# Windowed attention by 32 queries of four heads, with ACT, DVE and POOL in written order: one change to a fused trunk kernel on Trainium2

## The chip, the core and the metric

The kernel runs on one core of a Trainium2 chip as one launch. The core has a matrix engine (PE), a vector engine (DVE), a scalar engine (ACT), GpSimd (POOL) and SyncE (SP, here a queue that issues DMAs). The metric is the device time of an execution in microseconds, the median of several. A profile shows one execution; its span runs from the first to the last instruction, and a time "at 88.31" is counted from the start of the span.

## What is computed

One layer of a model with 512 positions and width 2048: a root-mean-square norm, attention in a window of 128 keys with 32 query heads of width 64 on 4 key and value heads, a bias by distance, one "sink" logit per head, a gate, an output projection, and then a gated embedding and a last norm.

```python
q, k, v, gate = jnp.split(h @ w_in, [2048, 2304, 2560], axis=-1)
...
scores = jnp.einsum('bnqhgd,bnjhd->bnhgqj', q, kb) * (64 ** -0.5) + bias
scores = jnp.where(mask, scores, jnp.finfo(jnp.float32).min)
m = jnp.maximum(scores.max(axis=-1, keepdims=True), sink)
e = jnp.exp(scores - m)
probs = e / (e.sum(axis=-1, keepdims=True) + jnp.exp(sink - m))
out = jnp.einsum('bnhgqj,bnjhd->bqhd', probs, vb)
...
x = x + (out * silu(gate)) @ w_out
x = x + (p @ ple_proj) * sigmoid(rmsnorm(x, ple_norm) @ ple_gate)
return rmsnorm(x, final_g)
```

## The kernel before

Matrices are multiplied in float32 split into a high part (rounded to the matrix engine's 4-byte format by a copy on ACT) and a low part (the rest, by a subtraction on DVE). `mm3` then issues three matmuls: high by high, high by low, low by high.

The stages follow each other on PE. First comes a loop of 16 steps over the width, which makes the first two query tiles, the keys and the values. Then 30 projections follow: 14 query tiles (two heads each) and 16 gate tiles, 16 steps of three matmuls each. Their weights come in 60 halves of 8 steps (half 0 to half 59; `wraw` is a half as loaded, `whi` and `wlo` its parts). `Weights.get(i)` makes the halves up to i + 2 as soon as half i is used, and `_make` loads a half by a DMA on SP's queue and splits it. Three buffers of each kind exist. The third stage, the output projection and the gate of the embedding by a scheme of seven products (`unit`), and the end are touched by one line only (`early`, which says after which step of `unit` a half of the last weights is split by `split_last`).

Attention is spread over the projections. The first projection stands ahead of it; then there are 64 blocks, 8 (`g`) for each of 8 groups of four heads (`d`). Turn i of the loop issues on PE the transposes of block i - 2 (`turn`), the weighing of the values of block i - 3 (`weigh`), the scores of block i (`scores`), and then about seven steps of the projections. A block before is 64 queries of two heads on the 128 partitions, twice (for the two pairs of heads), against 192 keys, or 128 in the first two blocks of a group. The keys lie as a high and a low half side by side, so a score matmul has 2 x 192 columns. `add` scales the product and adds the bias; of 192 keys a query sees 128, and since the two outer thirds exclude each other (the bias masks one), a maximum folds them together. Then come the maximum, the exponential with its sum, the reciprocal and the product with it.

Because keys of two blocks are folded, `weigh` needs beside the values V a second product: the masked weights (`own`) by differences of neighbouring value tiles (DV). `make_diff(n)` forms difference n on POOL and splits it by `split`; `spread_diff(n)` copies it into DV by four DMAs on SP's queue. `first_chores` does all three `make_diff` in turn 0, and in turns 1 to 3 the split of V[i] and `spread_diff(i)`. `own` is masked on POOL from the transposed weights `r`, and half of it is copied by ACT (the last line of `turn`). `weigh` ends every second block with two copies on ACT (`tmp`), each followed by an add on DVE.

Who sets the order: PE, SP and (in the attention) POOL run in the order in which the code is written. ACT and DVE have their instructions ordered by a scheduler before the kernel runs, apart from the stretch called `seam` and the end. On the chip each engine then runs its list in order. DMAs on SP's queue are issued in list order; one whose source isn't ready holds up all behind it. In that queue stand, at the start of attention: the bias of group 0, halves 3 and 4, a copy for `sum_weights`, spread 1, half 5, spread 2, half 6, and so on.

Of the kernel before, what the change touches and what calls it, by code (L numbers as in the profile page):

```python
# [19 lines left out]
S = 512  # L20
P = 128
# [9 lines left out]
UNITS = S // HB  # L31
BUCKETS = 32
# [7 lines left out]
PAD = 32  # L40
# [13 lines left out]
def trunk_kernel(ctx: ExitStack, tc: tile.TileContext, a: dict):  # L54
# [32 lines left out]
    class Weights:  # L87
# [4 lines left out]

        def add(self, src):
            self.srcs.append(src)
# [30 lines left out]
    sinkb = const.tile([P, PAIRS], F32, name="sinkb")  # L125
# [17 lines left out]
    sclq = const.tile([P, UNITS], F32, name="sclq")  # L143
# [24 lines left out]
    q_at = {int(0.5 + 3.516 * (c // 2)) - 2 + c % 2: c for c in range(2, PAIRS)}  # L168
# [15 lines left out]

    for k in range(KC):
        both = start_pool.tile([P, 2, 768], F32R, tag="w0s", name=f"w0s{k}")
# [50 lines left out]
        if k == 9:  # L237
            run(rsqrt_mean(rstd1, ssq1, D, "r1"))
            for e in range(2):
                for b in range(2):  # L240
                    nc.vector.tensor_scalar_mul(
                        sclq[HB * e : HB * e + HB].rearrange("p (n b) -> p n b", b=2)[:, :, b],
                        rstd1[HB * b : HB * b + HB], HD ** -0.5,
                    )

            rdram = tc.dram_tile([NB, P], F32, name="rdram")
            nc.gpsimd.dma_start(rdram.rearrange("t p -> p t"), rstd1)
            nc.gpsimd.dma_start(rb, rdram.rearrange("t p -> (t p)").partition_broadcast(P))
        if k == 10:
            for e in range(2):  # L250
                nc.sync.dma_start(sinkb[HB * e : HB * e + HB], a["sinks"][e].partition_broadcast(HB))
            nc.sync.dma_start(pn, a["ple_norm"])
# [5 lines left out]
    def evac_q(c, ps):  # L258

        q = Q[c] = kvq.tile([P, UNITS, 2, HB], F32R, tag="q", name=f"q{c}", bufs=4)  # L260
        halves = slice(0, 64), slice(64, 128)
        for e in range(2):
            src = ps[halves[e]].rearrange("p (g q) -> p g q", q=HB)
            hi, lo = q[halves[e], :, e], q[halves[1 - e], :, e]
            nc.scalar.copy(hi, src)
            nc.vector.tensor_sub(lo, src, hi.bitcast(F32))


    seam = ExitStack()
    seam.enter_context(  # L270
        tc.manual_schedule(engines={getattr(mybir.EngineType, v) for v in ("PE", "SP", "DVE", "Activation")})
    )
    for c in range(2):
        evac_q(c, q_ps[c])
# [4 lines left out]
    def make_key(h):  # L279

        t, e = divmod(h, 2)
        k = K[h] = kvq.tile([P, 2, S], F32R, tag="k", name=f"k{h}", bufs=2)
        same = slice(64 * e, 64 * e + 64)
        for o in (slice(0, 64), slice(64, 128)):
            nc.scalar.copy(k[o, 0], kt[t][same])
        for o in (slice(0, 64), slice(64, 128)):
            nc.vector.tensor_sub(k[o, 1], kt[t][same], k[same, 0].bitcast(F32))
# [4 lines left out]
    def split(dst, v):  # L292
        nc.scalar.copy(dst[:, :, 0, :], heads(v))
        nc.vector.tensor_sub(dst[:, :, 1, :], heads(v), dst[:, :, 0, :].bitcast(F32))

    nc.vector.tensor_mul(kt[0], kt_ps[0], rb)
    make_key(0)
# [8 lines left out]
    split(V[0], values[0])  # L306
    seam.close()
# [29 lines left out]
    DV = apool.tile([P, NB - 1, 2, KVH * 2 * HD], F32R, name="DV")  # L337
    diffs = {}

    def make_diff(n):  # L340
# [8 lines left out]
        split(dst.rearrange("p (h l d) -> p h l d", h=KVH, l=2), v)  # L349
# [7 lines left out]
    def first_chores(i):  # L357
        if i == 0:
            for n in range(1, NB):
                make_diff(n)  # L360
        if 1 <= i < NB:
            split(V[i], values[i])
            spread_diff(i)

    def load_bias(d):
        biases[d] = apool.tile([P, 2, P + HB], F32, tag="bias", name=f"bias{d}", bufs=2)
        for e in range(2):
            src = bass.AP(
                tensor=tdram.tensor, offset=tdram.offset + (4 * d + e) * TOEP + HB,
                ap=[[1, HB], [2 * TOEP, 2], [1, P + HB]],  # L370
            )
            nc.sync.dma_start(biases[d][HB * e : HB * e + HB], src)

    def scores(i):

        d, g = divmod(i, UNITS)
        odd = g % 2
# [4 lines left out]
        first = max(g - 2, 0) * HB  # L384
        n = P if g < 2 else P + HB
        s_ps = spsum.tile([P, 2, S], F32, tag="w", name=f"s{i}")
        for u in range(2):
            st = Q[2 * d + u][:, g].rearrange("p e q -> p (e q)")
            nc.tensor.matmul(s_ps[:, u, : 2 * n], st, key[:, :, first : first + n], start=True, stop=True)
        t = apool.tile([P, 2, 4 + P + HB], F32, tag="t", name=f"t{i}", bufs=4)  # L390
        seen = t[:, :, 65:194] if odd else t[:, :, 0:129]
        pr = t[:, :, 65:193] if odd else t[:, :, 1:129]
        sink = 193 if odd else 0
        nc.gpsimd.tensor_copy(t[:, :, sink], sinkb[:, 2 * d : 2 * d + 2])
        bias = biases[d][:, :, ::-1]

        def add(out, in0, in1):
            nc.vector.scalar_tensor_tensor(
                out=out, in0=in0, scalar=sclq[:, g : g + 1], in1=in1, op0=ALU.mult, op1=ALU.add
            )  # L400

        if g < 2:
            if g == 0:
                nc.gpsimd.memset(t[:, :, 65:129], MASKED)
            n = HB * (g + 1)
            out = pr[:, :, :n]
            add(out, s_ps[:, :, :n], bias[:, :, 192 - n :])
            add(out, s_ps[:, :, P : P + n], out)
        else:
            add(t[:, :, 1:193], s_ps[:, :, :n], bias)  # L410
            add(t[:, :, 1:193], s_ps[:, :, n : 2 * n], t[:, :, 1:193])
            ends = t[:, :, 1:65], t[:, :, 129:193]
            nc.vector.tensor_max(ends[odd], ends[0], ends[1])
        sm = apool.tile([P, 24], F32, tag="sm", name=f"sm{i}", bufs=4)
        nc.vector.tensor_reduce(sm[:, 0:2], seen, axis=AX.X, op=ALU.max, negate=True)  # L415
        for u in range(2):
            su = seen[:, u, :]
            nc.scalar.activation(su, su, AF.Exp, bias=sm[:, u : u + 1], accum_out=sm[:, 2 + u : 3 + u])  # L418
        nc.vector.reciprocal(sm[:, 4:6], sm[:, 2:4])
        for u in range(2):  # L420
            nc.scalar.mul(pr[:, u], pr[:, u], sm[:, 4 + u : 5 + u])
        T[i] = pr

    def turn(i):
# [5 lines left out]
        for u in range(2):  # L430
            nc.tensor.transpose(pt[:, u * P : (u + 1) * P], pr[:, u, :], ident)
        r = apool.tile([P, 2, 256], F32R, tag="r", name=f"r{i}", bufs=2)
        nc.scalar.copy(r[:, 0], pt)
        nc.vector.tensor_sub(r[:, 1], pt, r[:, 0].bitcast(F32))  # L434
        own = None
        if g >= 2:
# [9 lines left out]
            )  # L446
            here, there = slice(HB, P), slice(0, HB)
# [3 lines left out]
        PT[i] = (r, own)  # L451

    def weigh(i):
# [14 lines left out]
        if own is not None:  # L468
            nc.tensor.matmul(
                out, DV[:, n - 1, b, kv * 2 * HD : (kv + 1) * 2 * HD], own[:, 0], start=False, stop=True  # L470
            )
        if b:
# [5 lines left out]
        if g == UNITS - 1:  # L478
            for c in (2 * d, 2 * d + 1):
                weighed.add(c)  # L480
                if c in open_gates:
                    due.append(c)

    weighed, open_gates, due = set(), set(), []
    ah, al = {}, {}

    def gate_value():

        c = due.pop(0)
# [5 lines left out]
    def open_gate(c, ps):  # L495
# [3 lines left out]
        nc.vector.tensor_mul(x, ps, rb)  # L499
        nc.scalar.activation(ps, x, AF.Tanh, scale=0.5)  # L500
        nc.vector.scalar_tensor_tensor(out=x, in0=ps, scalar=1.0, in1=x, op0=ALU.add, op1=ALU.mult)
        open_gates.add(c)
        if c in weighed:
            due.append(c)
# [183 lines left out]
    def projections():  # L688
        for m, (kind, c) in enumerate(kinds):
            ps = bank(f"{kind}ps{c}", "p")  # L690
            for k in range(KC):
# [6 lines left out]
                if k == KC - 1:  # L698
                    if kind == "q":
                        evac_q(c, ps)  # L700
                    else:
                        g = c // 4
                        if c % 4 == 0:
                            gates[g] = quarter(f"gate{g}")
                        open_gate(c, ps)
# [3 lines left out]

    during = ExitStack()  # L710
    during.enter_context(
        tc.manual_schedule(engines={getattr(mybir.EngineType, v) for v in ("PE", "SP", "Pool")})
    )
    load_bias(0)
    for _ in range(KC):
        next(proj)
    blocks = TWOS * UNITS
    left = KC * (len(kinds) - 1)

    for i in range(blocks + 3):  # L720

        if 2 <= i < blocks + 2:
            turn(i - 2)
        if 3 <= i:
            weigh(i - 3)
        if i < blocks:
            scores(i)
            first_chores(i)
            if i in (6, 20, 36):
                make_key(1 + i // 16)  # L730
# [11 lines left out]
    while due:  # L742
        gate_value()
# [210 lines left out]
    early = {(5, 0, 3): 0, (5, 1, 2): 1, (5, 1, 3): 2, (3, 0, 1): 3, (3, 0, 3): 4, (3, 1, 0): 5, (3, 1, 2): 6}  # L954
# [161 lines left out]
def laid_out(i):  # L1116
# [24 lines left out]
        "sinks": f(np.asarray(i["swa_sinks"])[0].reshape(PAIRS, 2).T),  # L1141
# [19 lines left out]
```

## Time and profile before

| | |
|---|---|
| Median of 3 executions | 803.88 us (803.66 to 804.14) |
| The profiled execution: its own time | 804.26 us |
| Its span | 802.4 us |
| Mean granted clock of the matrix engine | 0.996 |
| First step loop, about | 4.7 to 72.4 us |
| Attention and projections, about | 72.4 to 449 us |
| DVE and ACT busy from 100 to 440 us | 261 and 226 of 340 us |

On the timeline a row gives the start, the duration, the engine, the line, the operation, output <- input, the shape and how many instructions are merged (x2); brackets show the idle time ahead and what ended it. Matmuls overlap, so their cost is the distance of their starts. A row of a group gives line, engine, operation, tiles, shape, count, then the busy time in us and the mean of one in ns, then the engine's idle time just before and what ended it. A row of DMA issues gives count, size of one and the median of us from issue to landing.

### The profile page before, as it was taken

Reading aid. Unit: us, or ns where it says so; the run is one execution under the profiler, and the core shown is the slowest. Engines: PE = TensorE matmul, PEld = TensorE weight load, DVE = VectorE, ACT = ScalarE, POOL = GpSimd, SP = SyncE. Lnnn points to the kernel's source line nnn. Section 1 sums busy time; section 2 is a strip of 40 time slices with the busy share of each in tenths; the row PEclk is TensorE's granted clock in tenths of the full one; section 3 lists DMA queues with packets and bytes.
Section 4 is the critical chain, followed back from the end, with each engine's and each line's share of the span. In section 5 each row is a group of like instructions: output and inputs, shape, how many; then the busy total and the mean of one; then the engine's idle time right before and its main releaser. Section 6 shows DMA issues by size and latency. Waiting matters only on the chain. (4 is left out here: it accounts for less than half of the span.)

```text
span 802.4 us, 10946 instructions
## 1 busy us (share of the span) xinstructions
PE 791.1 (99%) x3763; PEld 660.0 (82%) x3763; DVE 592.1 (74%) x970; ACT 500.5 (62%) x1041; POOL 110.1 (14%) x218
## 2 busy tenths in 40 slices
PE   9999999999999999999999999999999999999995
PEld 7888888888888888888888888888888888888785
DVE  4536886887777776777778897766646756989896
ACT  5624667676667666676666654655668656656855
POOL 0002213122122212112122200030000020200000
PEclk9999999999999999999999999999999999999998
DMA  8863678778687977868685369898513996785532
GB/s 318 327 172 101 183 241 215 228 202 233 172 220 215 218 215 199 221 177 246 159 219 132 105 233 348 333 275 248 195 46 92 372 216 197 156 229 182 182 107 105
DMA packets 45239, 165.15 MB, mean 206 GB/s; under 512 B 5936, under 2 KB 8112, under 8 KB 41344
## 3 DMA queue, kind: packets, MB, share of 16 engines
q1 hardware_dynamic: 38352, 130.59, 47.9%
q0 software_dynamic: 6832, 33.88, 22.4%
q8 instruction: 29, 0.48, 0.2%
q14 instruction: 26, 0.21, 0.1%
HBM read 158.63 MB, written 46.19 MB: 255 GB/s over the span
## 5 line engine op out<-in xcount | busy, mean ns | idle before, releaser
L576 DVE TENSOR_TENSOR blo<-braw,bhi 128x1024 fp32r<-128x1024 f32 x80 | 97.5, 1222 | 39.7 <-ACT bhi L575 39.4
L575 ACT CAST bhi<-braw 128x1024 fp32r<-128x1024 f32 x80 | 84.0, 1051 | 65.8 <-PE g L122 18.9
L122 PE MATMUL gps<-xh,wlo 128*128 128x512 f32 x256 | 100.1, 391 | 0.0
L121 PE MATMUL gps<-xl,whi 128*128 128x512 f32 x256 | 100.1, 391 | 0.0
L120 PE MATMUL gps<-xh,whi 128*128 128x512 f32 x256 | 99.8, 390 | 0.0
L107 DVE TENSOR_TENSOR wlo<-wraw,whi 128x1024 fp32r<-128x1024 f32 x60 | 73.3, 1221 | 20.8 <-ACT whi L106 19.7
L122 PE MATMUL qps<-xh,wlo 128*128 128x512 f32 x224 | 87.8, 392 | 0.0
L120 PE MATMUL o<-bhi,fho 128*128 128x512 f32 x224 | 87.7, 391 | 0.0
L121 PE MATMUL qps<-xl,whi 128*128 128x512 f32 x224 | 87.7, 391 | 0.0
L121 PE MATMUL o<-blo,fho 128*128 128x512 f32 x224 | 87.3, 390 | 0.0
L122 PE MATMUL o<-bhi,flo 128*128 128x512 f32 x224 | 87.2, 389 | 0.0
L120 PE MATMUL qps<-xh,whi 128*128 128x512 f32 x224 | 87.2, 389 | 0.0
L106 ACT CAST whi<-wraw 128x1024 fp32r<-128x1024 f32 x60 | 62.9, 1048 | 26.9 <-PE gps L121 10.6
L418 ACT ACTIVATE t<-t,sm 128x129 f32<-128x129 f32 x128 | 50.6, 397 | 45.9 <-DVE sm L415 45.6
L121 PE MATMUL g<-blo,fhg 128*128 128x512 f32 x192 | 75.0, 391 | 0.7 <-DVE blo L576 0.7
L120 PE MATMUL g<-bhi,fhg 128*128 128x512 f32 x192 | 75.1, 391 | 0.0
L122 PE MATMUL g<-bhi,flg 128*128 128x512 f32 x192 | 74.8, 390 | 0.0
L443 POOL TENSOR_SCALAR_AFFINE_SELECT own<-r 64x512 fp32r<-64x512 f32 (+1 forms) x48 | 34.1, 711 | 291.7 <-DVE r L434 286.2
L122 PEld LDWEIGHTS gps<-xh,wlo 128*128 128x128 f32 x256 | 48.0, 188 | 10.3
L576 DVE TENSOR_TENSOR blo<-grown,bhi 128x1024 fp32r<-128x1024 f32 x32 | 39.1, 1223 | 23.6 <-ACT bhi L575 21.9
L120 PEld LDWEIGHTS gps<-xh,whi 128*128 128x128 f32 x256 | 48.1, 188 | 8.9
L121 PEld LDWEIGHTS gps<-xl,whi 128*128 128x128 f32 x256 | 48.1, 188 | 8.9
(200 smaller groups left out, 1698.0 us busy)
## 6 DMA issues: line engine op xcount, KB each, us to landing
wraw<-in_w_gate_in SPq DMA_DIRECT2D x32, 512.0 KB, 5.6
wraw<-in_w_q SPq DMA_DIRECT2D x28, 512.0 KB, 4.5
w_out<-in_w_out POOLq DMA_DIRECT2D x24, 512.0 KB, 7.4
braw<-in_w_out SPq DMA_DIRECT2D x24, 512.0 KB, 4.3
braw<-in_ple_gate SPq DMA_DIRECT2D x24, 512.0 KB, 4.3
w_out<-in_w_out SPq DMA_DIRECT2D x16, 512.0 KB, 6.7
ple_gate<-in_ple_gate SPq DMA_DIRECT2D x16, 512.0 KB, 5.5
ple_gate<-in_ple_gate POOLq DMA_DIRECT2D x16, 512.0 KB, 7.2
```

The costliest lines, as they stand in the source:

```text
L106: nc.scalar.copy(hi, raw)
L107: nc.vector.tensor_sub(lo, raw, hi.bitcast(F32))
L120: nc.tensor.matmul(ps, sh, mh, start=first, stop=False, skip_group_check=more)
L121: nc.tensor.matmul(ps, sh, ml, start=False, stop=False, skip_group_check=more)
L122: nc.tensor.matmul(ps, sl, mh, start=False, stop=last, skip_group_check=more)
L418: nc.scalar.activation(su, su, AF.Exp, bias=sm[:, u : u + 1], accum_out=sm[:, 2 + u : 3 + u])
L443: nc.gpsimd.affine_select(out=flat(own), in_=flat(r).bitcast(F32), pattern=[[0, 8], [sign, HB]], compare_op=ALU.is_ge, fill=0.0, base=-HB ...
L575: nc.scalar.copy(hi, raw)
L576: nc.vector.tensor_sub(lo, raw, hi.bitcast(F32))
```

## The change

1. A block is now 32 queries of four heads, twice (two sets of 32 queries), against 160 keys; in the first two blocks of a group 32, 64, 96 and 128 keys. `evac_q` lays the four heads of a group in one tile and scales q itself, by two factors (`rb` holds the inverse norm of each position); `sclq` is gone, and the scores get only the bias. The fold is 32 columns wide. Probabilities go to a tile of their own (`pr`), with two halves exchanged where needed, and `turn` puts them back into blocks of 64 queries for `own` and `weigh`. The bias of a group comes by four DMAs rather than two.
2. ACT, DVE and POOL run in written order for the first two steps of the first loop (`front`) and from the end of that loop to the end of attention (`during`). `scores`, `turn` and `weigh` are generators that are advanced at fixed steps of the projections in a turn.
3. Splits are handed out by turns. A weight half asked for by `Weights.get` is put on a list (`todo`), of which one is made after the first step of each turn. The work on a finished projection is put on `chores`, one or two after the first step, one after the fifth. `first_chores` now forms difference i + 1 in turn i, splits difference i in turn i (high part after the first step, low part after the fifth), then issues spread i, and splits V[i - 2].
4. Query projections stand one place earlier (`q_at`). Four entries of `early` move by one or two steps.

```diff
         def get(self, i):
-            while len(self.made) <= min(i + self.ahead, len(self.srcs) - 1):
-                self._make(len(self.made))
+            while self.asked <= min(i + self.ahead, len(self.srcs) - 1):
+                self.todo.append(partial_of(self._make, self.asked))
+                self.asked += 1
+            while self.todo and not (self.apart and i < len(self.made)):
+                self.todo.pop(0)()
             return self.made[i]
...
-    def first_chores(i):
-        if i == 0:
-            for n in range(1, NB):
-                make_diff(n)
-        if 1 <= i < NB:
-            split(V[i], values[i])
-            spread_diff(i)
+    def first_chores(i, step):
+        if step == 0 and i < NB - 1:
+            make_diff(i + 1)
+        if step and 1 <= i < NB:
+            diffs[i][step - 1]()
+            if step == 2:
+                spread_diff(i)
+        if step and 1 <= i - 2 < NB:
+            split(V[i - 2], values[i - 2])[step - 1]()
...
-        first = max(g - 2, 0) * HB
-        n = P if g < 2 else P + HB
...
+        number = [min(2 * g + u + 1, 5) * QB for u in range(2)]
         for u in range(2):
-            st = Q[2 * d + u][:, g].rearrange("p e q -> p (e q)")
+            first, n = max(2 * g + u - 4, 0) * QB, number[u]
+            st = Q[d][:, 2 * g + u].rearrange("p h q -> p (h q)")
             nc.tensor.matmul(s_ps[:, u, : 2 * n], st, key[:, :, first : first + n], start=True, stop=True)
...
     for i in range(blocks + 3):
-        if 2 <= i < blocks + 2:
-            turn(i - 2)
-        if 3 <= i:
-            weigh(i - 3)
-        if i < blocks:
-            scores(i)
-            first_chores(i)
+        before, softmax = softmax, scores(i) if i < blocks else iter(())
+        turned = turn(i - 2) if 2 <= i < blocks + 2 else iter(())
+        value = weigh(i - 3) if 3 <= i else iter(())
+        next(turned, None)
+        next(value, None)
+        next(softmax, None)
+        next(turned, None)
+        next(before, None)
+        next(softmax, None)
+        first_chores(i, 0)
...
-        for n in range(todo):
-            if n == 5 and due:
-                gate_value()
-            next(proj)
+        for n in range(max(todo, 6)):
+            if n < todo:
+                next(proj)
+            if n == 0:
+                first_chores(i, 1)
+                some(W.todo)
+                some(chores, 2 if len(chores) > 3 else 1)
+            elif n == 2:
+                next(value, None)
+            elif n == 3:
+                next(turned, None)
+                next(softmax, None)
+            elif n == 4:
+                first_chores(i, 2)
+                some(chores)
+            elif n == 5:
+                next(softmax, None)
...
-    early = {(5, 0, 3): 0, (5, 1, 2): 1, (5, 1, 3): 2, (3, 0, 1): 3, (3, 0, 3): 4, (3, 1, 0): 5, (3, 1, 2): 6}
+    early = {(5, 0, 3): 0, (5, 1, 2): 1, (5, 1, 3): 2, (3, 0, 3): 3, (3, 1, 0): 4, (3, 1, 1): 5, (3, 1, 3): 6}
```

At step 3 of a turn (`n == 3`) `next(turned)` issues the ACT copy of `own`, after the `tmp` copies of `n == 2` and the weight half of `n == 0`.

More of the change, by code (lines that the diff above doesn't have):

```diff
@@ L31 @@
 UNITS = S // HB
+QB = P // 4
+KEYS = P + QB
 BUCKETS = 32
@@ L164, in rsqrt_mean @@
         nc.vector.tensor_mul(out, y, t)
-    q_at = {int(0.5 + 3.516 * (c // 2)) - 2 + c % 2: c for c in range(2, PAIRS)}
+    q_at = {int(0.5 + 3.516 * (c // 2)) - 3 + c % 2: c for c in range(2, PAIRS)}
     kinds, g = [], 0
@@ L258, in evac_q, with scaled, split @@
     def evac_q(c, ps):
-        q = Q[c] = kvq.tile([P, UNITS, 2, HB], F32R, tag="q", name=f"q{c}", bufs=4)
+        d, u = divmod(c, 2)
+        if u == 0:
+            Q[d] = kvq.tile([P, S // QB, 4, QB], F32R, tag="q", name=f"q{d}", bufs=2)
         halves = slice(0, 64), slice(64, 128)
[L262 to L271, printed above, removed]
-    )
-    for c in range(2):
-        evac_q(c, q_ps[c])
+        def scaled():
+            nc.vector.scalar_tensor_tensor(out=ps, in0=ps, scalar=HD ** -0.5, in1=rb, op0=ALU.mult, op1=ALU.mult)
+        def split(low):
+            for e in range(2):
+                src = ps[halves[e]].rearrange("p (s q) -> p s q", q=QB)
+                hi, lo = Q[d][halves[e], :, 2 * u + e], Q[d][halves[1 - e], :, 2 * u + e]
+                if low:
+                    nc.vector.tensor_sub(lo, src, hi.bitcast(F32))
+                else:
+                    nc.scalar.copy(hi, src)
+        return scaled, partial_of(split, False), partial_of(split, True)
+    during = ExitStack()
+    during.enter_context(
+        tc.manual_schedule(
+            engines={getattr(mybir.EngineType, v) for v in ("PE", "SP", "DVE", "Activation", "Pool")}
+        )
+    )
+    first_q = [evac_q(c, q_ps[c]) for c in range(2)]
+    for part in (first_q[0][0], first_q[1][0], *first_q[0][1:], *first_q[1][1:]):
+        part()
     kt = [kvq.tile([P, S], F32, name=f"kt{t}") for t in range(2)]
@@ L283, in make_key, with part @@
         same = slice(64 * e, 64 * e + 64)
[L284 to L287, printed above, removed]
+        def part(low):
+            for o in (slice(0, 64), slice(64, 128)):
+                if low:
+                    nc.vector.tensor_sub(k[o, 1], kt[t][same], k[same, 0].bitcast(F32))
+                else:
+                    nc.scalar.copy(k[o, 0], kt[t][same])
+        return partial_of(part, False), partial_of(part, True)
     heads = lambda v: v.rearrange("p (h d) -> p h d", h=KVH)
@@ L305, in trunk_kernel @@
         )
-    split(V[0], values[0])
-    seam.close()
+    for part in split(V[0], values[0]):
+        part()
     misc = quarter("misc")
@@ L391, in scores @@
[L391 to L400, printed above, removed]
-        if g < 2:
[L403 to L408, printed above, removed]
-        else:
[L410 to L413, printed above, removed]
+        W = KEYS + 2
@@ new lines, in scores, with two @@
+        t = apool.tile([P, 2, W], F32, tag="t", name=f"t{i}", bufs=3)
+        at = t[:, 0, 0:1]
+        def two(of, stride, n):
+            return bass.AP(tensor=at.tensor, offset=at.offset + of, ap=[at.ap[0], [stride, 2], [1, n]])
+        late = QB if g >= 2 else 0
+        seen = [t[:, 0, 0 : P + 1], t[:, 1, 1 + late : P + 2 + late] if late else t[:, 1, 0 : P + 1]]
+        both = two(0, W + 1 + late if late else W, P + 1)
+        pr = [t[:, u, 1 + late * u : 1 + late * u + P] for u in range(2)]
@@ L420, in scores @@
+        T[i] = apool.tile([P, 2, P], F32, tag="pr", name=f"pr{i}", bufs=3)
         for u in range(2):
-            nc.scalar.mul(pr[:, u], pr[:, u], sm[:, 4 + u : 5 + u])
-        T[i] = pr
+            out, src = T[i][:, u], pr[u]
+            if late and (g + u) % 2:
+                out = out.rearrange("p (h k) -> p h k", h=2)[:, ::-1]
+                src = src.rearrange("p (h k) -> p h k", h=2)
+            nc.scalar.mul(out, src, sm[:, 4 + u : 5 + u])
     def turn(i):
@@ L446, in turn @@
             )
+        PT[i] = (r, own)
+        yield
+        if own is not None:
             here, there = slice(HB, P), slice(0, HB)
@@ L688, in projections @@
     def projections():
+        parts = {}
         for m, (kind, c) in enumerate(kinds):
+            while any(v in chores for v in parts.get(m - 2, ())):
+                chores.pop(0)()
             ps = bank(f"{kind}ps{c}", "p")
@@ L698, in projections @@
                 if k == KC - 1:
[L699 to L705, printed above, removed]
+                    if kind == "g" and c % 4 == 0:
+                        gates[c // 4] = quarter(f"gate{c // 4}")
+                    parts[m] = (evac_q if kind == "q" else open_gate)(c, ps)
@@ L706, in projections, with some @@
+                    chores.extend(parts[m])
                 yield
     proj = projections()
[L710 to L713, printed above, removed]
     load_bias(0)
-    for _ in range(KC):
+    W.apart = True
+    for n in range(KC):
         next(proj)
+        if n % 4 == 3 and W.todo:
+            W.todo.pop(0)()
     blocks = TWOS * UNITS
     left = KC * (len(kinds) - 1)
+    def some(of, n=1):
+        for _ in range(min(n, len(of))):
+            of.pop(0)()
@@ L741, in trunk_kernel @@
         pass
-    while due:
-        gate_value()
+    while chores:
+        some(chores)
     during.close()
```

108 lines of the change are left out of this document (67 added, 41 removed).

## The prediction

> **What bounds the kernel now.** I read the page first, then the order of the matrix engine's instructions in one turn of the attention loop, then the DMA queue of SP at the start of that loop.
>
> ```profile
> PE 791.1 (99%) x3763; PEld 660.0 (82%) x3763; DVE 592.1 (74%) x970; ACT 500.5 (62%) x1041; POOL 110.1 (14%) x218
> ```
>
> The matrix engine (PE) is busy for 791.1 of 802.4 us, so a microsecond goes only where PE has fewer columns or waits less, and any new wait of PE is added in full. One turn of attention on the timeline of PE:
>
> ```profile
> 200.71 0.38 PE L431 MATMUL pt<-ident,t 128*128 128x128 f32 x2
> 200.85 0.48 PE L467 MATMUL o<-r,V 128*128 128x256 f32 x2
> 201.17 0.28 PE L469 MATMUL o<-own,DV 128*128 128x256 f32 x1
> 201.29 0.52 PE L389 MATMUL s<-k,q 128*128 128x384 f32 x2
> 201.64 0.39 PE L120 MATMUL qps<-xh,whi 128*128 128x512 f32 x1
> ```
>
> Starts follow each other without a hole. The two score matmuls take 201.64 - 201.29 = 0.35 us of PE; a durations column that reads 0.52 overlaps with the next. There is no wait to remove here, only columns. The start of the loop is another matter. SP's queue there:
>
> ```profile
> 85.71 2.45 SPq L355 DMA_DIRECT2D DV<-diffs  x4
> 88.20 0.59 SPq L99 DMA_DIRECT2D wraw<-in_w_q  x1
> 88.89 2.39 SPq L355 DMA_DIRECT2D DV<-diffs  x4
> 91.38 0.53 SPq L99 DMA_DIRECT2D wraw<-in_w_q  x1
> 91.95 0.53 SPq L544 DMA_DIRECT2D w_out<-in_w_out  x1
> 92.58 2.47 SPq L355 DMA_DIRECT2D DV<-diffs  x4
> ...
> 98.00 1.56 SPq L372 DMA_DIRECT2D bias<-tdram  x2
> ```
>
> Each spread of the value differences (DV, four issues) stands ahead of one load of projection weights: half 5 goes out at 88.20, half 6 at 91.38, half 7 behind the third spread. A queue issues in order, so a weight half can't leave before the differences ahead of it are split. Before, all three were split early, and that cost nothing.
>
> **The change, part by part.**
>
> *Scores.* Per pair of 64-query blocks the columns fall from 2x384 to 2x320, and in the first two blocks of a pair of heads (two pairs) from 1024 to 640 columns. A pair of 256 columns shows a duration of 0.40 (row below), one of 384 shows 0.52: 0.12 us for 256 columns, 0.47 ns each. So 48 pairs save 128 x 0.47 = 0.06 us, 2.9 us. For the 8 first groups it is 384 x 0.47 = 0.18 us at most, 1.4 us in all, and nothing if a matmul of 64 or 128 columns costs as much as one of 256; two transposes of 128 columns start 0.07 us apart (200.71 to 200.85), so small ones are cheaper, and I take 0.9. Sum 3.8 us (2.5 to 4.3).
>
> *Values and weights in turns: the main term.* The changed kernel writes the order of ACT and DVE out. Value difference 1 is split in turn 1, 2 in turn 2, 3 in turn 3, its low part at the fifth step of the turn; the weight half due in the turn is split at the first step. So on DVE the order is: low part of half 5, then of difference 2; half 6, then difference 3. On SP the order is still: spread 2, then half 6; spread 3, a w_out copy, four bias loads, then half 7. This closes a ring: half 5 must land before difference 2 can be split, that before spread 2, that before half 6 goes out, and so on. Its rows:
>
> ```profile
> 85.20 0.41 DVE L294 TENSOR_TENSOR diffs<-diffs 128x256 fp32r<-128x256 f32 x1
> 85.53 0.34 DVE L398 SCALAR_TENSOR_TENSOR t<-s,sclq,bias 128x128 f32<-128x128 f32 x1
> 85.91 0.35 DVE L398 SCALAR_TENSOR_TENSOR t<-s,sclq,t 128x128 f32<-128x128 f32 x1
> 86.30 0.42 DVE L415 TENSOR_REDUCE sm<-t 128x2 f32<-128x258 f32 x1
> 86.64 0.68 DVE L501 SCALAR_TENSOR_TENSOR gate<-gps,gate 128x512 f32<-128x512 f32 x1
> ```
>
> ```profile
> 88.31 0.40 PE L389 MATMUL s<-k,q 128*128 128x256 f32 x2
> ```
>
> ```profile
> L107 DVE TENSOR_TENSOR wlo<-wraw,whi 128x1024 fp32r<-128x1024 f32 x60 | 73.3, 1221 | 20.8 <-ACT whi L106 19.7 <-PE pt L431 0.7
> L106 ACT CAST whi<-wraw 128x1024 fp32r<-128x1024 f32 x60 | 62.9, 1048 | 26.9 <-PE gps L121 10.6 <-PE qps L121 10.0 <-DMA wraw<-in_w_gate_in 5.9
> ...
> L477 DVE TENSOR_TENSOR u<-o,tmp 64x256 f32<-64x256 f32 x64 | 26.8, 418 | 2.9 <-ACT tmp L476 1.9
> ...
> L476 ACT COPY tmp<-o 64x256 f32<-64x256 f32 x64 | 23.5, 368 | 12.7 <-DVE u L477 11.7
> ...
> L266 DVE TENSOR_TENSOR q<-qps,q 64x512 fp32r<-64x512 f32 x32 | 22.0, 689 | 9.0 <-ACT q L265 8.4
> ```
>
> ```profile
> wraw<-in_w_gate_in SPq DMA_DIRECT2D x32, 512.0 KB, 5.6
> wraw<-in_w_q SPq DMA_DIRECT2D x28, 512.0 KB, 4.5
> w_out<-in_w_out POOLq DMA_DIRECT2D x24, 512.0 KB, 7.4
> ```
>
> On the clock of the profiled execution: the scores of turn 1 are out at 88.31 + 0.40 = 88.7. DVE does four adds (0.35 each), the maximum (0.42), the gate (0.68) and the low part of difference 1 (0.41): 91.6. Spread 1 starts 0.1 later, as at 85.61 to 85.71, and half 5 goes out 2.49 after it (85.71 to 88.20), at 94.2. A half lands after 4.5 to 5.6 us, 7.4 for a transfer of the same size in traffic; I take 5.0 here and 5.6 where a w_out copy goes just ahead. Half 5: 99.2. High and low part (1.05, 1.22): 101.5. Difference 2: 101.9. Spread 2 and the copy (2.49, and 0.63 from 91.95 to 92.58): half 6 goes out at 105.1, lands at 110.7, low part at 113.0. Where was it due?
>
> ```profile
> 104.81 0.51 PE L389 MATMUL s<-k,q 128*128 128x384 f32 x2
> ...
> 110.42 0.28 PE L469 MATMUL o<-own,DV 128*128 128x256 f32 x1
> ```
>
> Turn 4 begins its projection steps at 104.81 + 0.35, and half 6 is needed four steps of three matmuls later (0.23 each): 107.9. Its projection also needs the PSUM bank of the first query projection, whose low parts (two of 0.69) stand behind half 6, difference 3 and value tile 1 (0.41 each) on DVE: 115.2. PE waits from 107.9 to 115.2.
>
> The ring goes on while PE waits. Difference 3 is split at 113.4; spread 3, the copy and four bias loads (1.56 / 2 = 0.78 each) put half 7 out at 119.7, landing at 125.3. In turn 4 ACT's written order has the high part of half 7, then two copies of the output (tmp), then the copy of the masked weights (own) of block 2. So own, ready on POOL long before, stands behind a DMA: high part 126.35; the low part and one add on DVE (1.22, 0.42), which the second tmp copy waits for, 128.0; tmp and own (0.37 each, the same shape) 128.8. PE needs own in turn 5, at 110.42 before; now 128.9. That is 18.5 us, the first wait inside it. If every half lands in 4.5 us and neighbours on DVE overlap by 1 us in all, it is 14.8; at 7.4 us each, 24.5. I keep the middle.
>
> From turn 6 halves 8 and later have no spread ahead of them and go out three halves early, so the ring ends. What PE saved in turns 0 to 4 is lost in the wait: 3.4 of the 3.8 us count.
>
> *Clock.* PE has stood still for long and may come back slow.
>
> ```profile
> 0.85 3.52 PE L135 MATMUL warm_ps<-const-bfloat16-1.0 128*128 128x128 bf16 x37 [0.85 <-PEq L1151]
> ```
>
> At the start 37 matmuls of 128 columns took 3.52 us, 95 ns each; later 512 columns take 0.23, 57 ns for 128. If 3.5 us after the last wait run at that rate, 3.5 x (1 - 57/95) = 1.4 us are lost; nothing if the clock holds through 10 us of idling. I take 1.4. [...] No row of this trace has such a gap before its end, so nothing here confirms the fall.
>
> *Late splits of the last stage.* Four entries move one or two steps later.
>
> ```profile
> 745.13 1.23 DVE L584 TENSOR_TENSOR low<-grown,last 128x1024 fp32r<-128x1024 f32 x1 [0.26 <-ACT last L583]
> ```
>
> ```profile
> 750.87 0.39 PE L120 MATMUL g<-bhi,fhg 128*128 128x512 f32 x1
> 751.93 0.50 PE L121 MATMUL g<-blo,fhg 128*128 128x512 f32 x1 [0.68 <-DVE blo L576]
> ```
>
> PE's next start is 1.06 after 750.87 in place of 0.23, behind a low part that the split at 745.13 held up by 1.2 us. Without it DVE is 1.2 us earlier: 0.8 us, and 0.1 of a smaller one; I take 0.9 (0 to 1.0, 0 if the moved split is now late for the next half).
>
> *Nothing each, with their cover.* Scaling q (16 x 0.68 us on DVE) replaces the scaling in the adds, which also lose 64 columns a query block; DVE's 74% covers the difference, and PSUM of the first query tile is still free before PE returns to it. The first two steps in written order let PE start a few tenths sooner in step 0, but step 1 is then met by its own loads: 0 to 0.4, taken as 0. Order in the steady turns: in even turns own stands behind two tmp copies that alternate with DVE, with some 1 us to spare by my adding up; I take 0.5 (0 to 4).
>
> *Sum,* against the profiled execution's 804.26 us: 804.26 + 18.5 - 3.4 + 1.4 - 0.9 + 0.5 = 820.4. That execution lay 0.4 above the median of 803.88, so 820.0.
>
> **The rivals.** *The loads hide (faster).* If halves 6 and 7 arrive in time, only the savings stay: 803.9 - 3.8 - 0.9 + 0.5 = 799.7. For it: before, the same queue order did no harm. Against it: without any landing a round of the ring is 1.05 + 1.22 + 0.41 + 0.1 + 2.49 + 0.63 = 5.9 us, and PE uses a half in 8 steps, 5.5 us, plus 0.8 of attention in most turns. It decides for faster only where landing is under a microsecond; the shortest group shows 4.5.
>
> *Only the first wait.* If own does not wait behind half 7, PE loses 107.9 to 115.2, 7.3 us: 803.9 + 7.3 + 1.4 - 3.4 - 0.9 + 0.5 = 808.8. Against it: the order on ACT is fixed.
>
> *The steady turns stall too.* If own or the transposed weights come 0.3 us late in the 30 even turns that remain, 9 us come on top: 829. For it: tmp and its add already make ACT wait 11.7 us (row of L476). Against it: DVE and ACT are far from full.
>
> **How the numbers follow.** The forecast has 0.75, only the first wait 0.08, stalling turns 0.08, hidden loads 0.07, a wait that just pays back the savings 0.02. Landing sets the range: the ends 14.8 and 24.5 with the other bounds give 812 to 827, which leaves most of the two outer rivals out. A change within 0.2% (1.6 us) can't be told from none: 0.02; faster 0.07, slower 0.91.
>
> **What would show it.** Spreads on SP near 92, 102 and 113 in place of 85.7, 88.9 and 92.6; loads of halves 5, 6 and 7 near 94, 105 and 120; two holes of PE, near 108 to 115 and 117 to 129, the second ended by own; a score pair of 0.29; no wait near the late split. Wrong, if PE runs through from 88 to 130, if the spreads go out near 86 to 93, or if the time is lost evenly over all turns.

## The result, and the profile after

| | before | after |
|---|---|---|
| Median | 803.88 us (803.66 to 804.46, 5 executions) | 825.45 us (823.74 to 825.73, 5 executions) |
| Ratio, 95% interval | | 1.026 (1.0248 to 1.0272) |
| Profiled execution: its time, its span | 804.26, 802.4 us | 823.74, 821.1 us |
| Mean granted clock of PE | 0.996 | 0.985 |

The change costs 21.6 us by the medians. The profiled execution of after is the fastest of its five, 19.48 us above that of before, and the accounts below are made with that one. First the page of after: the busy shares, the clock of PE in 40 slices of 20.5 us, and the group of the high parts of the weight halves.

```profile
PE 793.1 (97%) x3763; PEld 662.7 (81%) x3763; DVE 587.9 (72%) x1014; ACT 495.9 (60%) x1041; POOL 111.7 (14%) x234
...
PEclk9999978999999999999999999999999999999998
...
L110 ACT CAST whi<-wraw 128x1024 fp32r<-128x1024 f32 x60 | 62.3, 1039 | 22.9 <-DMA wraw<-in_w_gate_in 15.9
```

PE went from 99% to 97%: it waits, and that is the loss. Its clock dips in slices 6 and 7, near 102 to 144 us. ACT waited 15.9 us for the loads of weight halves; before, DMA stood at 5.9 us in this group. The starts of the scores on PE, turn by turn, say where the time went:

| turn | before, us | after, us | difference | step |
|---|---|---|---|---|
| 0 | 83.29 | 82.42 | -0.87 | |
| 4 | 104.81 | 103.74 | -1.07 | |
| 5 | 110.54 | 123.41 | +12.87 | +13.94 |
| 6 | 116.27 | 131.15 | +14.88 | +2.01 |
| 22 | 207.02 | 220.86 | +13.84 | |
| 23 | 212.75 | 230.00 | +17.25 | +3.41 |
| 38 | 297.95 | 314.08 | +16.13 | |
| 39 | 303.69 | 324.58 | +20.89 | +4.76 |
| 40 | 309.62 | 330.82 | +21.20 | +0.31 |
| 63 | 440.19 | 459.72 | +19.53 | |

Everywhere else after gains some 0.07 us a turn on average. So there are two places: turns 4 to 6, and the two pairs of turns around 22 and 38.

*Turns 4 to 6.* SP's queue of after, which answers to the one shown of before:

```profile
90.19 2.43 SPq L387 DMA_DIRECT2D DV<-diffs  x4
92.67 0.59 SPq L103 DMA_DIRECT2D wraw<-in_w_q  x1
99.94 2.38 SPq L387 DMA_DIRECT2D DV<-diffs  x4
...
103.01 0.58 SPq L103 DMA_DIRECT2D wraw<-in_w_gate_in  x1
110.57 2.38 SPq L387 DMA_DIRECT2D DV<-diffs  x4
...
113.64 1.97 SPq L406 DMA_DIRECT2D bias<-tdram  x4
115.66 0.42 SPq L103 DMA_DIRECT2D wraw<-in_w_gate_in  x1
```

Before, the three spreads stood at 85.71, 88.89 and 92.58, one right behind the other. Now 9.75 and 10.63 us lie between them, and halves 6 and 7 go out behind spreads 2 and 3 (the rows left out are the w_out copies of 0.60 us). The queue keeps to its list: it issues nothing from 93.26 to 99.94 and from 103.59 to 110.57, while the head of the list is a spread. ACT with its list of turn 4, on the timeline:

```profile
119.64 1.04 ACT L110 CAST whi<-wraw 128x1024 fp32r<-128x1024 f32 x1 [6.18 <-DMA wraw<-in_w_gate_in]
120.71 0.37 ACT L529 COPY tmp<-o 64x256 f32<-64x256 f32 x1
122.30 0.36 ACT L529 COPY tmp<-o 64x256 f32<-64x256 f32 x1 [1.23 <-DVE u L530]
122.57 0.40 ACT L503 CAST own<-own 64x256 fp32r<-64x256 f32 x1
```

The copy of `own` ends 3.3 us after half 7 has landed, behind it in ACT's list. And PE:

```profile
106.55 0.39 PE L129 MATMUL qps<-xh,wlo 128*128 128x512 f32 x1
112.39 0.77 PE L127 MATMUL gps<-xh,whi 128*128 128x512 f32 x1 [5.45 <-DVE q L281]
...
116.65 0.78 PE L519 MATMUL o<-r,V 128*128 128x256 f32 x2
123.03 0.58 PE L521 MATMUL o<-own,DV 128*128 128x256 f32 x1 [5.60 <-ACT own L503]
...
123.94 0.63 PE L127 MATMUL gps<-xh,whi 128*128 128x512 f32 x1
124.37 0.63 PE L128 MATMUL gps<-xl,whi 128*128 128x512 f32 x1
```

Two waits, 5.45 us for the query's low parts and 5.60 us for `own`. After each, matmuls of 512 columns start 0.43 us apart (123.94 to 124.37) in place of 0.23: the granted clock was 0.50 from 112.40 to 116.40 and from 123.00 to 127.80, and 0.99 in the 3.60 us after that.

*Turns 22 and 38.* The end of the first of these two gaps on PE, and DVE's list ahead of it:

```profile
225.03 0.39 PE L129 MATMUL gps<-xh,wlo 128*128 128x512 f32 x1
228.62 0.50 PE L127 MATMUL qps<-xh,whi 128*128 128x512 f32 x1 [3.21 <-DVE q L281]
```

```profile
220.34 1.38 DVE L311 TENSOR_TENSOR k<-kt,k 64x512 fp32r<-64x512 f32 x2
221.63 0.68 DVE L274 SCALAR_TENSOR_TENSOR qps<-qps,rb 128x512 f32<-128x512 f32 x1
...
223.96 0.42 DVE L483 TENSOR_TENSOR r<-pt,r 128x256 fp32r<-128x256 f32 x1 [1.44 <-ACT r L482]
...
225.93 1.22 DVE L111 TENSOR_TENSOR wlo<-wraw,whi 128x1024 fp32r<-128x1024 f32 x1
227.18 1.39 DVE L281 TENSOR_TENSOR q<-qps,q 64x512 fp32r<-64x512 f32 x2
```

A new projection needs the PSUM bank (the memory in which its matmuls add up) of the last but one, here that of query 7, whose low parts come at 227.18. They stand behind the low part of key 2 (220.34): `make_key` puts its two parts on the list `chores` in turn 20 ahead of query 7's three, and with one or two parts popped after the first step of a turn and one after the fifth, the low parts slip from the fifth step of turn 21 to the first of turn 22. The projection that needs the bank starts six steps later.

*The scores.* A turn of after on PE, answering to the one shown of before:

```profile
204.02 0.46 PE L424 MATMUL s<-k,q 128*128 128x320 f32 x2
204.32 0.39 PE L127 MATMUL qps<-xh,whi 128*128 128x512 f32 x1
```

0.30 us a pair in place of 0.35.

### The profile page after: what moved, and what is told of

Same layout as the page of the kernel before. It is cut to its first block, busy times and chain, and to the rows that moved or that the text cites. A ratio compares the mean times of both kernels' runs of the same rounds, so it can differ in the third digit from the quotient of the medians.

```text
span 821.1 us, 10983 instructions
## 1 busy us (share of the span) xinstructions
PE 793.1 (97%) x3763; PEld 662.7 (81%) x3763; DVE 587.9 (72%) x1014; ACT 495.9 (60%) x1041; POOL 111.7 (14%) x234
## 5 line engine op out<-in xcount | busy, mean ns | idle before, releaser
L127 PE MATMUL gps<-xh,whi 128*128 128x512 f32 x256 | 101.5, 397 | 5.5 <-DVE q L281 5.5
L110 ACT CAST whi<-wraw 128x1024 fp32r<-128x1024 f32 x60 | 62.3, 1039 | 22.9 <-DMA wraw<-in_w_gate_in 15.9
L493 POOL TENSOR_SCALAR_AFFINE_SELECT own<-r 64x512 fp32r<-64x512 f32 (+1 forms) x48 | 32.4, 675 | 283.6 <-DVE r L483 272.2
L483 DVE TENSOR_TENSOR r<-pt,r 128x256 fp32r<-128x256 f32 x64 | 27.1, 424 | 57.9 <-ACT r L482 56.9
L529 ACT COPY tmp<-o 64x256 f32<-64x256 f32 x64 | 23.5, 367 | 57.3 <-DVE u L530 56.5
```

What stands on the lines that cost most here:

```text
L110: nc.scalar.copy(hi, raw)
L127: nc.tensor.matmul(ps, sh, mh, start=first, stop=False, skip_group_check=more)
L483: nc.vector.tensor_sub(rl, src, rh.bitcast(F32))
L493: nc.gpsimd.affine_select(out=flat(own), in_=flat(r).bitcast(F32), pattern=[[0, 8], [sign, HB]], compare_op=ALU.is_ge, fill=0.0, base=-HB ...
L529: nc.scalar.copy(tmp[o], ops[x, :, :, e, :])
```

## The experiments

Kernels in one table were compared with the kernel before on the same chip: its median was 804.23 us in the first group, 805.06 in the second.

| | median, us | ratio to before, 95% interval |
|---|---|---|
| loads_ahead | 809.0 | 1.006 (1.0047 to 1.0074) |
| keys_23_39 | 816.04 | 1.0143 (1.0127 to 1.0158) |
| loads_and_keys | 799.4 | 0.9944 (0.9932 to 0.9957) |
| diffs_first | 824.01 | 1.0245 (1.0231 to 1.0259) |
| halves_last (second group) | 834.48 | 1.0365 (1.0351 to 1.0379) |
| loads_keys_26_42 (second group) | 807.45 | 1.0024 (1.0012 to 1.0036) |
| before_front (second group) | 804.21 | 0.9989 (0.998 to 0.9997) |
| before_late (second group) | 804.16 | 0.999 (0.9981 to 0.9999) |

### Loads ahead of the spreads

```diff
             while self.asked <= min(i + self.ahead, len(self.srcs) - 1):
+                self.load(self.asked + 1)
                 self.todo.append(partial_of(self._make, self.asked))
```

> The load of a weight half goes out on SP when the half is asked for, one half earlier, so halves 5, 6 and 7 no longer stand behind spreads 1, 2 and 3 on SP; nothing else is moved. My theory (the ring through SP and DVE): the waits of whi at 97.2, 107.9 and 119.6 us and PE's two gaps at 106.5 to 112.4 and about 117.4 to 123.0 us go, and the slow clock behind them; the steps of +13.94 and +2.01 us at turns 5 and 6 go with them, so about 825.4 - 15.9 = 809.5 us (808 to 811); the gaps at 225 and 318 us stay. Rival 1 (the loads are late because DMA is busy, not because of their place on SP): within 2 us of 825. Rival 2 (only one wait hangs on the order, another takes its place): 815 to 819.

Measured: 809.0 us. SP's queue of this kernel, and ACT's high parts of halves 6 and 7:

```profile
90.63 2.43 SPq L388 DMA_DIRECT2D DV<-diffs  x4
93.11 0.58 SPq L103 DMA_DIRECT2D wraw<-in_w_gate_in  x1
97.29 2.38 SPq L388 DMA_DIRECT2D DV<-diffs  x4
...
100.35 0.58 SPq L103 DMA_DIRECT2D wraw<-in_w_gate_in  x1
```

```profile
100.08 1.05 ACT L110 CAST whi<-wraw 128x1024 fp32r<-128x1024 f32 x1
105.91 1.05 ACT L110 CAST whi<-wraw 128x1024 fp32r<-128x1024 f32 x1 [0.22 <-DMA wraw<-in_w_gate_in]
```

Half 6 now leaves at 93.11 instead of 103.01, half 7 at 100.35 instead of 115.66, and ACT waits 0.22 us for it instead of 6.18. PE has no gap here: its scores stand at -0.63 us against before in turn 4 and at -0.78 in turn 6. One line, and nothing but the place of the loads on SP: the ring is shown, and its price is the 16 us of turns 5 and 6.

### Keys put on the list later

```diff
-        if i in (6, 20, 36):
+        if i in (6, 23, 39):
```

> The parts of keys 2 and 3 are put on the list of chores at turns 23 and 39 instead of 20 and 36, so they no longer stand ahead of the evacuations of query projections 7 and 11. My theory: PE's gaps at 225 and 318 us are its wait for the low parts of those two queries, whose bank the second next projection needs; by the order of the list the low parts then go out 9 steps of a projection ahead of that need instead of 6, as in the turns that show no gap. Steps of 3.49, 4.84 and 0.39 us go: about 825.4 - 8.7 = 816.7 us (815.5 to 818). Rival (those turns are overfull on DVE whatever the keys do): 824 to 826, with the gaps where they were, or moved to turns 25 and 41.

Measured: 816.04 us, and no gap at turns 22 and 38 (differences of +15.47 and +15.42 in turns 22 and 23, +14.50 and +14.44 in 38 and 39). The rival, that these turns are overfull whatever the keys do, is out.

### Both

> Both edits together. If the two theories hold, and the two costs are independent: 825.4 - 15.9 - 8.7 = 800.8 us (799 to 802.5), which is under the kernel before (803.9) by the front's 0.9, the shorter scores (0.06 to 0.08 us a turn) and the late splits. Rival (a further wait was covered by these two): 804 to 810.

Measured: 799.4 us, 0.56% below before. In ratios to before the two edits take 0.020 and 0.0117 off 1.026, together 0.0317, and both in one kernel 0.0316: the costs are independent, within the 0.0015 or so by which each ratio is uncertain. The page of this kernel:

```profile
PE 786.9 (99%) x3763; PEld 658.6 (83%) x3763; DVE 588.2 (74%) x1014; ACT 495.8 (62%) x1041; POOL 110.7 (14%) x234
...
PEclk9999999999999999999999999999999999999998
```

PE is at 99% again, with 4.2 us less work than in the kernel before (791.1), and the clock doesn't dip before the end. Its scores go from -0.04 us in turn 0 to -4.67 in turn 63: what the change gains in the attention once nothing waits.

### Differences ahead of the half

```diff
-            diffs[i][step - 1]()
-            if step == 2:
+            if step == 1:
+                diffs[i][0]()
+                diffs[i][1]()
                 spread_diff(i)
```

> The other link of the ring is cut, and only in part: both parts of difference n and its spread come ahead of the weight half of the same turn on ACT, DVE and SP. Loads stay where they are. By the ring theory spread 2 then no longer waits for half 5, but spread 3 still waits for the low part of half 5 (landed about 100 us), so half 6 goes out at about 103 to 104 us as now, and half 7, with no spread ahead of it any more, at about 106 to 108 us instead of 115.7: the first gap of PE (5.8 us, with the slow clock behind it) stays, the second (5.6 us and 2.0 of slow clock) goes: 825.4 - 7.6 = 817.8 us (816 to 820). Rival (any cut of the ring frees all): 809 to 811. Rival (the place on SP alone matters, not what the spread waits for): 824 to 826.

Measured: 824.01 us, 6 more than I expected, and at the edge of the last rival's range. SP's queue, and the end of PE's longest wait (x8 are spreads 1 and 2; the second is held up within the 8.47 us):

```profile
90.31 8.47 SPq L387 DMA_DIRECT2D DV<-diffs  x8
98.83 0.59 SPq L103 DMA_DIRECT2D wraw<-in_w_q  x1
...
108.54 2.39 SPq L387 DMA_DIRECT2D DV<-diffs  x4
110.97 0.59 SPq L103 DMA_DIRECT2D wraw<-in_w_gate_in  x1
...
114.18 0.42 SPq L103 DMA_DIRECT2D wraw<-in_w_gate_in  x1
```

```profile
119.67 0.76 PE L127 MATMUL gps<-xh,whi 128*128 128x512 f32 x1 [6.49 <-DVE q L281]
```

The third round went as expected: half 7 leaves 3.2 us behind half 6, with no spread between. But spread 2 now stands ahead of half 5 too, and waits until turn 2's work on DVE is done (the difference's low part at 95.96), so half 5 leaves at 98.83 instead of 92.67, and half 6 at 110.97 instead of 103.01. I had counted half 5 as landed by 100 us. PE still has two waits, 2.89 us for half 5 itself (at 104 us) and the 6.49 above, and its scores of turn 5 stand at +13.72 us against before, no better than the +12.87 of the changed kernel. So the time is that of the last rival (the place on SP alone matters), and the trace bears it out but for one thing: what a spread waits for counts too, since spread 2 was issued by 98.78 instead of 102.32. That gained nothing here, because it put one more load behind a spread.

### Halves behind the rest of the turn

```diff
             if n == 0:
                 first_chores(i, 1)
-                some(W.todo)
                 some(chores, 2 if len(chores) > 3 else 1)
...
             elif n == 4:
                 first_chores(i, 2)
                 some(chores)
+                some(W.todo)
```

> The changed kernel with one line moved: in every turn the split of a weight half comes behind the own copies, the tmp copies and one chore, at the end of the turn's steps, instead of ahead of them. The ring stays: halves 6 and 7 are as late as before (landed about 108 and 120 us). Ring theory: the two things that PE waited for, the query's low parts and the own copy, no longer stand behind a late half, so what is late next is half 7 itself, which PE needs at about 113.5 us and has at about 121: one gap of some 7.5 us and 1.9 us of slow clock in place of two gaps: 825.4 - 6.5 = 819 us (817 to 821). Rival (the halves had slack, only the queue order on ACT and DVE made them matter): 809 to 811. Rival (another instruction behind the half takes the place): 823 to 827.

Measured: 834.48 us, 15 above my expectation and 7 above the range of the last rival (another instruction takes the place), whose mechanism it has. PE's waits around the ring:

```profile
101.11 0.77 PE L477 MATMUL pt<-ident,pr 128*128 128x128 f32 x2 [2.25 <-ACT pr L468]
112.65 0.77 PE L477 MATMUL pt<-ident,pr 128*128 128x128 f32 x2 [4.29 <-ACT pr L468]
124.12 0.62 PE L477 MATMUL pt<-ident,pr 128*128 128x128 f32 x2 [3.23 <-ACT pr L468]
126.74 0.58 PE L521 MATMUL o<-own,DV 128*128 128x256 f32 x1 [1.66 <-ACT own L503]
```

The halves are as late as before, and now ACT's last product of the softmax (`pr`) stands behind them, which PE needs at the head of the next turn: three waits, one for each late half, and a rest for `own`. By turn 6 that makes +18.59 us. Later, three waits of 1.5 us for `own` came up (at 176, 272 and 369 us) that the changed kernel doesn't have. I had asked what the moved line frees, and not what stands behind it at its new place.

### The keys at two other turns

```diff
-        if i in (6, 20, 36):
+        if i in (6, 26, 42):
```

(on top of the early loads)

> The kernel with early loads, with the parts of keys 2 and 3 put on the list at turns 26 and 42 instead of 23 and 39. By the order of the list query 9's low parts then go out 5 steps of a projection ahead of the need of their bank (8 with the keys at 23), at turn 29; query 7's and 11's go out 9 ahead. My theory (a wait for the bank when the low parts go out 6 steps ahead or less): the gaps at turns 22 and 38 are gone, one new gap at turn 29 (about 250 us), of 3 to 5 us with 0 to 1.9 us of slow clock behind it, and none at turn 45: 799.4 + 3 to 6 = 802.5 to 805.5 us. Rival (turns 22 and 38 themselves are overfull): gaps there as in the changed kernel, 807 to 809. Rival (keys anywhere but there are free): 799 to 800.

Measured: 807.45 us. PE's waits:

```profile
246.29 0.39 PE L522 MATMUL o<-own,DV 128*128 128x256 f32 x1 [1.47 <-ACT own L504]
253.32 0.53 PE L128 MATMUL gps<-xh,whi 128*128 128x512 f32 x1 [2.93 <-DVE q L282]
```

The time alone would fit the rival of overfull turns (807 to 809), but its gaps aren't there: those at 22 and 38 are gone, and the new one is where the list puts it, at the start of a projection in turn 29, ended by a query's low parts. I had not seen the smaller waits for `own`, 1.47 us here and 1.45 at 342 us: a key's low part (1.38 us on DVE, at 239.37 and 335.82), behind which DVE works without a hole, also holds up the add (245.13 and 341.31) that ACT's second `tmp` copy waits for. That took the time 2 us above my range (0.8 of it is in before as well: 805.06 on this chip, 804.23 on that of the first group). What a key costs is what stands behind it, not the turn as such.

### The front and the late splits alone

The kernel before, with its first two steps in written order:

```diff
+        if k == 0:
+            front.enter_context(tc.manual_schedule(engines={...}))
+        if k == 2:
+            front.close()
```

> The kernel before with its first two steps alone in written order, as in the changed kernel. The profiled run of the changed kernel reaches its first scores 0.87 us earlier than that of the kernel before, other runs of the same front only 0.02 to 0.43 earlier. My theory: the written order is worth 0 to 0.4 us: 803.8 to 804.2 us, first scores 0 to 0.4 us earlier. Rival: 0.9 us: 803.3.

Measured: 804.21 against 805.06, 0.0011 of the time with an interval of 0.0003 to 0.002: 0.2 to 1.6 us. It can't tell 0.4 from 0.9. The first scores of this execution came 0.23 us earlier than in that of before; in the kernel with the late splits alone, whose front is that of before, 0.44 us earlier. So single executions differ here by as much as the front could be worth, and the 0.87 of the changed kernel's profile isn't its proof.

```diff
-    early = {..., (3, 0, 1): 3, (3, 0, 3): 4, (3, 1, 0): 5, (3, 1, 2): 6}
+    early = {..., (3, 0, 3): 3, (3, 1, 0): 4, (3, 1, 1): 5, (3, 1, 3): 6}
```

> The kernel before with the table of the late splits alone as in the changed kernel. My theory: the wait of 0.8 us at about 751 us goes, and nothing else changes: 804.2 - 0.85 = 803.4 us (803.2 to 803.8). Rival (the splits collide elsewhere, or the order of the end gives it back): 804 to 805.

Measured: 804.16 against 805.06, an interval of 0.1 to 1.5 us, which alone proves little. The place of the wait is clearer. PE there:

```profile
750.62 0.49 PE L121 MATMUL g<-blo,fhg 128*128 128x512 f32 x1
750.96 0.40 PE L122 MATMUL g<-bhi,flg 128*128 128x512 f32 x1
```

The matmul that started 1.06 us behind the one before it (751.93) now follows 0.22 behind (750.40 to 750.62). The wait is gone.

## Why the prediction was right, and where it was not

The sum of the prediction against the profiled execution, by steps:

| step | predicted, us | measured, us |
|---|---|---|
| the ring, up to PE's own matmul | +18.5 (14.8 to 24.5) | +13.94 |
| clock behind it | +1.4 | +2.01 |
| scores | -3.4 | -4.24 |
| order in the steady turns | +0.5 (0 to 4) | +8.69 |
| late splits | -0.9 | -0.83 |
| front | 0 (0 to -0.4) | -0.87 |
| around the span | | +0.78 |
| sum | +16.1 | +19.48 |

The measured terms are steps of the turn table. The forecast of the ring counts from before's 110.42, so what was saved until turn 4 is lost within it; counted like this, the scores of turn 5 come 12.87 us late, in which the front and the 0.20 of turns 0 to 4 are contained. To the three steps of turns 23, 39 and 40 (8.48) are added the 0.07 a turn that were gained besides; scores are -0.20 up to turn 4 and -4.04 from turn 6 on; late splits are what the span (+18.7) lacks of turn 63's +19.53, a rest that contains whatever else differs in the last stage; the front is turn 0.

**The ring was right, its size was too large.** Every link was found: spreads at 90.2, 99.9 and 110.6 (forecast 92, 102, 113), halves at 92.7, 103.0 and 115.7 (94, 105, 120), waits ended by the query's low parts and by `own`. `loads_ahead` proves the order on SP as the cause. What was mis-sized: `own`'s matmul came at 123.03 and not 128.9, 12.6 us behind before's 110.42 where the lower end of that term was 14.8. Half 7 left 4.0 us earlier than reckoned: 1.5 are due to spread 1, which left at 90.19 and not at 91.7, and 1.2 to the bias loads, which took 1.97 / 4 = 0.49 us each and not the 0.78 of the larger ones before. From the start of the issue to the high part the halves took 4.56, 4.86 and 3.98 us (5.0, 5.6 and 5.6 reckoned); for half 7 alone that is 1.6.

**The step that failed is the order in the steady turns.** The prediction looked for a wait for `own` behind two `tmp` copies, found 1 us to spare and set 0.5. That wait didn't come. What came stood in the same list of chores that the change introduces: a key ahead of a query, twice, 8.69 us in all. The term's upper end was 4, and its rival ("in the 30 even turns that remain") had the loss spread over the even turns, where it sat in two places. The profile of before could have priced it (0.69 us for each low part), but only the order of the list says when it falls due.

**These two errors, -5.6 us (12.87 for 18.5) and +8.2, go opposite ways**, so that the sum came within 3.4 us of the trace is partly luck. The range doesn't hang on it: with the keys out of the way (`keys_23_39`) 816.04 us were measured, 4 us below the forecast and still between 812 and 827.

**Clock.** It fell, and the forecast of 1.4 was near the 2.01 of turn 6, though not by its own reasoning: the 37 matmuls at the start, whose 95 ns it took for a slow clock, ran at a granted clock of 1.00 (0.85 to 4.37 in before), so no run shows that rate as one of a slow clock. What the runs showed in its place is the clock of 0.50, at which 512 columns took 0.43 us and not 0.23. What follows the two key gaps of the changed kernel (columns: stretch, length, busy time of PE, PEld, DVE, ACT and POOL, granted clock of PE, share of DMA, GB/s) shows that not every gap costs it:

```profile
228.62:232.22 3.60, 3.60 (x19) 3.07 (x20) 2.26 (x6) 3.15 (x10) 0.81 (x2) 1.00 1.02 325
322.22:325.92 3.70, 3.70 (x13) 3.16 (x14) 1.90 (x5) 3.25 (x10) 0.84 (x4) 0.54 0.94 289
```

After 3.20 us of idling the clock held at 1.00, after 3.58 it was 0.54 for the next 3.7 us. The last section has two more of these gaps.

**Scores.** The pair costs 0.30 (0.29 forecast). The gain of 4.24 lies within the 2.5 to 4.3 of the term; the 4.63 of `loads_and_keys` lie just above it. The prediction kept 3.4, since turns 0 to 4 were to lose theirs in the wait, which is right for the 0.20 gained there.

**The front** stays open between 0 and 0.9 us. Of the late splits the mechanism was right, since the wait is gone; their size is known only roughly, since the rest behind turn 63 is 0.1 to 0.9 us in the six later kernels with the same table.

## What to carry to other kernels

When an order is written out by hand, follow each in-order queue around: a DMA that waits for an engine, ahead of a load for which that same engine waits, is a ring, and each round costs a landing (here 9.75 and 10.63 us a round, 4.56 and 4.86 of them from the issue of a half to its high part). For every instruction that may wait, list what stands behind it on its engine and when each of those is due; a list of chores handed out one by one is such a queue, and a single large chore put in front can make the last one miss its step. Moving the late instruction only chose who waited for it (`halves_last`, 834.48 us); making it early, by one line that sends the load off when it is asked for, took the wait away (`loads_ahead`, 809.0 us).

## What the runs showed of the hardware

The length of a gap alone doesn't tell whether PE's clock falls behind it. In the changed kernel PE idled for 3.20 us up to 228.62, and the clock then held at 1.00 for 3.60 us (the row 228.62:232.22 above). Two gaps of nearly the same length, in `loads_ahead` and in `diffs_first`, and what followed them (the same columns):

```profile
210.08:213.31 3.23, 0.01 (x1) 0.01 (x1) 3.12 (x6) 0.42 (x2) 0.63 (x2) 0.98 0.74 122
213.31:216.70 3.39, 3.39 (x11) 2.96 (x12) 1.45 (x5) 2.83 (x10) 0.38 (x1) 0.51 0.69 193
216.70:220.10 3.40, 3.40 (x16) 2.81 (x15) 3.30 (x7) 1.91 (x6) 1.46 (x5) 1.00 0.61 106
```

```profile
224.18:227.42 3.24, 0.01 (x2) 0.01 (x1) 3.13 (x6) 0.42 (x2) 0.64 (x2) 1.00 0.66 124
227.42:228.35 0.93, 0.93 (x5) 0.75 (x6) 0.50 (x2) 0.51 (x2) 0.00 (x0) 1.00 0.95 189
228.35:231.77 3.42, 3.42 (x13) 2.94 (x12) 2.44 (x8) 3.31 (x10) 1.57 (x5) 0.51 0.79 293
231.77:235.00 3.23, 3.23 (x15) 2.65 (x14) 1.81 (x4) 1.49 (x5) 0.21 (x3) 0.99 0.87 162
```

Behind the 3.23 us of `loads_ahead` the clock was 0.51 for 3.39 us and then 1.00. Behind the 3.24 us of `diffs_first` it was 1.00 for the first 0.93 us of work, then 0.51 for 3.42 us: here it fell after work had begun again. In the two longer gaps of the changed kernel it fell while PE still idled: stretches of 0.1 us show 0.50 from 110.8 to 117.6 and from 121.0 to 127.9, where the gaps began at 106.94 and 117.43, so 3.9 and 3.6 us into each.

A gap of 3.20 to 3.58 us thus cost its own length, or some 1.7 us more where the clock fell. The 1.7 is an estimate from the rows: 0.49 of 3.39 and of 3.42 us, and 0.46 of the 3.70 us behind the gap of 3.58. What decides between the two isn't shown.
